# A hybrid SSD and attention block on one core: another order of rows in attention's second heads, and a later place for its first transposes

## The chip, the cores and the metric

The kernel runs on one core of one Trainium2 chip. The metric is the device time of one execution in microseconds. Three runs of the kernel before took 1223.24, 1229.5 and 1222.28 us; the median is 1223.24 us. One more execution was profiled.

## The reference, cut to what matters

One block of an encoder, on 1024 positions of width 1024, in float32:

```python
h = rms_norm(x, pre_mix_gain)
z, xbc, dt_raw, q, k, v = split(h @ w_in)              # 512, 1024, 8, 512, 512, 512 columns
xbc = silu(causal_depthwise_conv(xbc, conv_w, conv_b))  # 4 taps
y_ssd = gated_norm(ssd_scan(...) + d_skip * xs, z)      # 8 heads, a state of 128
# stick-breaking attention, 8 heads of 64; for each query block of 128 rows:
zz = q_block @ k[:end].T / 8
log_1mb = where(s < t, log_sigmoid(-zz), 0)
after = reverse_cumsum(log_1mb) - log_1mb
w = where(s < t, exp(log_sigmoid(zz) + after), 0)
o = w @ v[:end]
mix = concat([y_ssd, rms_norm_per_head(o)]) @ w_out
x = x + rms_norm(mix, post_mix_gain)
f = (silu(h2 @ w_gate) * (h2 @ w_up)) @ w_down          # h2 = rms_norm(x, pre_ffn_gain), width 2816
x = x + rms_norm(f, post_ffn_gain)
```

In attention a row of weights is as long as the positions that come before it, so the work of a query block grows with its place.

## The kernel before, in words

The sequence is reversed on the host, so that query block 0 has the longest rows (1024 keys) and block 7 the shortest (128). All large products are done in three passes of split operands (mm3, lines 77 to 79): high by high, high by low, low by high.

**Two streams.** The first part of the kernel runs two streams of work that one core shares. `fill` (line 887) projects the input: for each tile of 128 columns, `proj` (line 249) does two halves of 512 positions, each with 8 x 3 products, and gives way after every second of the 8 input blocks. At blocks 3 and 5 of the first half it fetches the next tile's weights (line 258). The order of tiles is PLAN: pair 1's q, k and v, then the conv tiles x0 to x5, pair 2's, x7, x6, the SSD recurrence (which runs beside), pair 3's, then the gates z and the first output loads. A conv tile also leaves four taps of work for VectorE to the side (lines 394 to 406), and it records the last product of each of its halves in the list `x_mm` (line 392).

`attention` (line 630) is the other stream. It has four pairs j of two heads h. A unit (j, h, g) is two neighbouring query blocks, 2g and 2g + 1: g = 0 has rows of 1024 and 896 keys, g = 1 of 768 and 640, g = 2 of 512 and 384, g = 3 of 256 and 128. For pairs 0 to 2 a head's units go from g = 0 to g = 3; in pair 3 the two heads alternate, from g = 3 to g = 0.

**One unit.** `weigh` (line 577) makes one row block of weights: products of q and k into zp (lines 589, 590), two sigmoids on ScalarE into sn and sp (591, 592), a mask on GpSimd (596), a running product along the row on VectorE (the scan, 597), and a product on VectorE (598) that leaves the weights in sp. `turn` (line 601) transposes the two rows' blocks on TensorE into tp (608); ScalarE copies that to wh (612) and VectorE takes the rest to wl (613). `mix_v` (616) multiplies by v into o. A unit has 4 - g turns, the first with 3 transposes, the others with 4. While unit i is turned, unit i + 1 is weighed: its first row in unit i's first turn, its second after the last turn. The first row of a new head first loads that head (`prep_head`, six loads on SyncE's queue), and for a new pair waits until that pair's v is emitted (`ready`, line 637). When a pair's last unit is done, `norm_o` (625) stores and squares its output.

**The order.** `merge` (line 690) takes from attention or from fill by a table of paces (PACE, line 43): attention goes on while its own count of VectorE work, as a share of A_ALL, is at or under the pace for the fill's count of TensorE work. A stream that gives way with (0, 0) has to wait, and the other goes on. What `merge` emits earlier has the higher priority; a scheduler then sets the final order on each engine by its own estimates, so an instruction that it takes for ready can be put ahead of one that it takes for waiting. On the chip each engine runs its own list in that order. `tc.issue_after(ins)` puts the instructions traced inside it, those on the engine of `ins`, behind `ins` in that engine's list. The second row of the first unit is already ordered so, behind the last product of x0's first half (line 656).

Of the kernel before, what the change touches and what calls it, by code (L numbers as in the profile page):

```python
# [47 lines left out]
def tile_hybrid_block(  # L48
# [20 lines left out]
    last_mm, evac, last_dve = [None], [None], [None]  # L69
# [6 lines left out]
    def mm3(ps, ah, al, bh, bl, start, stop, more=False):  # L76
        T.matmul(ps, lhsT=ah, rhs=bh, start=start, stop=False, skip_group_check=more)  # L77
        T.matmul(ps, lhsT=ah, rhs=bl, start=False, stop=False, skip_group_check=more)  # L78
        last_mm[0] = T.matmul(ps, lhsT=al, rhs=bh, start=False, stop=stop, skip_group_check=more)  # L79
# [9 lines left out]
    def psum(tag, name, shape=None, dt=F32):  # L89
        return psP.tile(shape or [P, 512], dt, tag=tag, name=name, bufs=BANKS[tag])  # L90
# [77 lines left out]
    def load_w_half(col, name, dh):  # L168
        raw = wp.tile([P, 4, P], F32, tag="wraw", name=f"wr_{name}", bufs=2)
        nc.sync.dma_start(raw, w_in_v[:, 4 * dh : 4 * dh + 4, col : col + P])  # L170
        hi = wp.tile([P, 4, P], F32R, tag="whi", name=f"wh_{name}")
        lo = wp.tile([P, 4, P], F32R, tag="wlo", name=f"wl_{name}")

        with tc.issue_after(first_sg[-1].ins) if name == "x1" else nullcontext():
            split(hi, lo, raw)
        return hi, lo
# [8 lines left out]
    def fetch_w(half=None):  # L185

        if cols:
            name, col = cols[0]
            w = w_tiles.setdefault(name, [])
            for dh in range(2) if half is None else (half,):  # L190
                w.append(load_w_half(col, name, dh))
            if len(w) == 2:
                cols.pop(0)

    def w_of(w, d):
        hi, lo = w[d // 4]
        return hi[:, d % 4, :], lo[:, d % 4, :]
# [51 lines left out]
    def proj(name, evac, dve):  # L249
        if name not in w_tiles:  # L250
            fetch_w()
        w = w_tiles.pop(name)
        for n in range(2):
            ps = psum("mm", f"pj_{name}")
            for d in range(ND):
                mm3(ps, *w_of(w, d), hh[d][n], hl[d][n], d == 0, d == ND - 1)
                if n == 0 and d in (3, 5):
                    fetch_w(d // 2 - 1)
                if d % 2 and d < ND - 1:
                    yield 1.3, 0  # L260
            evac(n, ps, slice(512 * n, 512 * n + 512))
            yield 1.3, dve
# [37 lines left out]
    v_first, k_evac, x_mm, decayed = [], [], [], []  # L300
# [245 lines left out]
    def prep_head(j, st, h):  # L546

        hsl = slice(64 * h, 64 * h + 64)
        kh = att.tile([P, S], F32R, tag="kh", name="kh")
        kl = att.tile([P, S], F32R, tag="kl", name="kl")  # L550
        qq = att.tile([P, S], F32R, tag="qq", name="qq")
        for half in range(2):
            dst = slice(64 * half, 64 * half + 64)
            nc.sync.dma_start(f32(qq[dst, :]), qkv_d[j]["q"][half][hsl, :])
        for half in range(2):
            dst = slice(64 * half, 64 * half + 64)
            nc.sync.dma_start(f32(kh[dst, :]), qkv_d[j]["k"][0][hsl, :])
            nc.sync.dma_start(f32(kl[dst, :]), qkv_d[j]["k"][1][hsl, :])
        return kh, kl, qq
# [17 lines left out]
    def weigh(head, qb):  # L577

        kh, kl, qq = head
        W = S - P * qb  # L580
        sn = att.tile([P, S + 1], F32, tag="sn", name="sn")
        sp = att.tile([P, S], F32, tag="sp", name="sp", bufs=3)
        G.memset(sn[:, 0:1], 1.0)
        off = 0
        qsl = slice(P * qb, P * qb + P)
        for cw_ in CH[W]:
            zp = psum("z", "zp", [P, 512])
            ksl = slice(P * qb + off, P * qb + off + cw_)
            T.matmul(zp[:, 0:cw_], lhsT=qq[:, qsl], rhs=kh[:, ksl], start=True, stop=False)
            T.matmul(zp[:, 0:cw_], lhsT=qq[:, qsl], rhs=kl[:, ksl], start=False, stop=True)  # L590
            A.activation(sn[:, 1 + off : 1 + off + cw_], zp[:, 0:cw_], AF.Sigmoid, scale=rqn[:, qb : qb + 1])  # L591
            sg = A.activation(sp[:, off : off + cw_], zp[:, 0:cw_], AF.Sigmoid, scale=rqp[:, qb : qb + 1])  # L592
            if len(first_sg) < 2:
                first_sg.append(sg)
            off += cw_
        G.affine_select(sp[:, 0:P], sp[:, 0:P], [[1, P]], ALU.is_gt, 0.0, base=0, channel_multiplier=-1)  # L596
        V.tensor_tensor_scan(sn[:, 1 : 1 + W], sn[:, 1 : 1 + W], smask[:, 0:W], 1.0, ALU.mult, ALU.max)  # L597
        V.tensor_tensor(sp[:, 0:W], sp[:, 0:W], sn[:, 0:W], ALU.mult)  # L598
        return sp

    def turn(ws, g, jj):

        kb = 2 * g + 2 * jj
        tp = psum("px", "tp", [P, 512])
        blocks = [(kb + 1, 0), (kb + 1, 1), (kb, 0)] + ([(kb, 1)] if jj else [])
        for i, (k, a) in enumerate(blocks):
            co = P * (k - 2 * g - a)
            T.transpose(tp[:, P * i : P * i + P], ws[a][:, co : co + P], ident)  # L608
        n_ = P * len(blocks)
        wh = att.tile([P, 512], F32R, tag="wh", name="wh", bufs=3)  # L610
        wl = att.tile([P, 512], F32R, tag="wl", name="wl", bufs=3)
        A.copy(wh[:, 0:n_], tp[:, 0:n_])  # L612
        V.tensor_tensor(wl[:, 0:n_], tp[:, 0:n_], f32(wh[:, 0:n_]), ALU.subtract)  # L613
        return kb, n_, wh, wl
# [10 lines left out]
    def norm_o(j, o_sb, n):  # L625
        sl = slice(512 * n, 512 * n + 512)
        nc.sync.dma_start(y_d[n][4 + j], o_sb[:, sl])
        mean_sq(o_sb[:, sl], sel2, 0, (j, j + 4), n, HD)

    def attention(st):  # L630


        units = [(j, h, g) for j in range(3) for h in range(2) for g in range(4)]
        units += [(3, h, g) for g in (3, 2, 1, 0) for h in range(2)]
        heads, vvs, osb, ws = {}, {}, {}, {}

        def ready(j):
            while "v" not in st[j] or not decayed:
                yield 0, 0

        def weights(i, a):
            if i < len(units):
                j, h, g = units[i]
                if (j, h) not in heads:
                    yield from ready(j)
                    heads[(j, h)] = prep_head(j, st[j], h)
                    yield 0, 0.1
                ws[(i, a)] = weigh(heads[(j, h)], 2 * g + a)
                W = P * (8 - 2 * g - a)
                yield W / 1200, W / 480 + 0.1  # L650

        yield from weights(0, 0)

        while not x_mm:
            yield 0, 0
        with tc.issue_after(x_mm[0].ins):
            yield from weights(0, 1)
        for i, (j, h, g) in enumerate(units):
            if j not in vvs:
                vvs[j] = prep_v(j, st[j])  # L660
                osb[j] = stg.tile([P, S], F32, tag="osb", name=f"osb{j}")
                yield 0.9, 1.2
            w = (ws.pop((i, 0)), ws.pop((i, 1)))
            o = psum("o", "o", [P, 256])
            n_j = 4 - g
            lag = None
            for jj in range(n_j):
                cur = turn(w, g, jj)
                yield 0.4, 0.6
                if jj == 0:  # L670
                    yield from weights(i + 1, 0)
                if lag is not None:
                    mix_v(o, vvs[j], h, lag, jj == 1, False)
                    yield 0.4, 0
                lag = cur
            yield from weights(i + 1, 1)
            mix_v(o, vvs[j], h, lag, n_j == 1, True)
            tmp = t2.tile([HD, 256], F32, tag="t2", name="otmp")
            A.copy(tmp, o[64:128, :])
            V.tensor_tensor(osb[j][64 * h : 64 * h + 64, 256 * g : 256 * g + 256], o[0:64, :], tmp, ALU.add)  # L680
            yield 0.4, 0.3
            if j < 3 and h == 1 and g == 3:
                norm_o(j, osb[j], 0)
                norm_o(j, osb[j], 1)
                yield 1.7, 0
            if j == 3 and h == 1 and g in (2, 0):
                norm_o(j, osb[j], g // 2)
                yield 0.9, 0
# [198 lines left out]
    def fill():  # L887
# [7 lines left out]
        yield from flush()  # L895

    merge(attention(st), fill())

    left_a.close()
# [427 lines left out]
    for p in range(last + 1):  # L1327
        while p not in done or done[p] < 7:
            pump(1 + LOOK)
            gate(step(p))  # L1330
            if p == last:
                i = done[p]
# [136 lines left out]
```

## Time and profile before

| what | value |
|---|---|
| median of three runs | 1223.24 us |
| profiled execution, its own time | 1221.82 us |
| its span, first to last instruction | 1220.1 us |
| TensorE busy | 1189.0 us, 97% |
| VectorE busy | 928.7 us, 76% |
| ScalarE busy | 588.9 us, 48% |
| mean granted clock of TensorE | 0.996 |

Attention's transposes run from 100.5 to 479.3 us of the span. Busy time counts an engine from the start to the end of its instructions, with overlaps once. A wait is named by the instruction that waited and by what released it. PE is TensorE, DVE is VectorE, ACT is ScalarE, POOL is GpSimd, SP is SyncE; L598 is line 598 of the kernel.

### The profile page before, as it was taken

The page shows a single profiled execution, that of the slowest core. Times are in us where ns is not written, and L with a number is a line of the kernel's source. Part 1 is how long each engine was busy: PE and PEld are TensorE (multiplying, and loading weights), DVE is VectorE, ACT ScalarE, POOL GpSimd, SP SyncE. Part 2 cuts the span into 40 slices and gives each one's busy share as a digit, 9 for nine tenths or more (in the row PEclk, how much of TensorE's full clock was granted, in tenths as well). Part 3 has the DMA queues.
Part 4 walks back from the last instruction along what each step waited for, and adds up shares of the span by engine and source line. Part 5 has one row for each costly group of instructions (what it writes and reads, how often), then busy time and mean ns, then how long its engine had stood idle before and what let it go on. Part 6 is the DMA issues. An engine that isn't in the chain of part 4 may idle for free.

```text
span 1220.1 us, 16382 instructions
## 1 busy us (share of the span) xinstructions
PE 1189.0 (97%) x5649; PEld 967.9 (79%) x5649; DVE 928.7 (76%) x1527; ACT 588.9 (48%) x1124; POOL 90.9 (7%) x232
## 2 busy tenths in 40 slices
PE   9999899999999998999999999999999999999997
PEld 7787777787887776688888888888888888888885
DVE  7468889778897988678898755566555559998877
ACT  7246656555654766455652323333233335444453
POOL 0011110101120100011200000000000000000000
PEclk9999999999999999999999999999999999999999
DMA  6794333445657424767963322322223397233246
GB/s 195 196 344 132 96 104 99 142 103 162 177 154 210 147 70 159 223 194 229 315 188 123 100 78 78 104 72 84 78 78 104 100 347 270 83 108 120 93 135 238
DMA packets 141414, 183.99 MB, mean 151 GB/s; under 512 B 10670, under 2 KB 96394, under 8 KB 141332
## 3 DMA queue, kind: packets, MB, share of 16 engines
q1 hardware_dynamic: 130016, 151.94, 40.8%
q0 software_dynamic: 7424, 25.17, 5.5%
q10 hardware_dynamic: 3892, 5.84, 1.3%
q8 instruction: 44, 0.72, 0.3%
q14 instruction: 38, 0.31, 0.1%
HBM read 133.00 MB, written 49.90 MB: 150 GB/s over the span
## 4 chain that ended last, share of the span: by engine, by line
PE 62%; DVE 5%; issue 2%; DMA 1%; ACT 1%; POOL 0%; SPq 0%; DVEq 0%; ACTq 0%; POOLq 0%
PE pd L78 5%; PE pd L77 5%; PE pd L79 5%; PE po L79 2%; PE po L78 2%; PE po L77 2%; PE peu L79 2%; PE pag L79 2%; PE peg L79 2%; PE pcu L79 2%; PE pcg L79 2%; PE pau L79 2%; PE pag L77 2%; PE pag L78 2%; PE pcg L77 2%
## 5 line engine op out<-in xcount | busy, mean ns | idle before, releaser
L73 ACT CAST flhi<-fraw 128x512 fp32r<-128x512 f32 x98 | 60.2, 622 | 153.4 <-PE pcg L78 36.6
L78 PE MATMUL pd<-folo,fohi 128*128 128x512 f32 x260 | 101.2, 389 | 0.0
L79 PE MATMUL pd<-fohi,folo 128*128 128x512 f32 x260 | 101.2, 389 | 0.0
L77 PE MATMUL pd<-fohi 128*128 128x512 f32 x260 | 101.2, 389 | 0.0
L597 DVE TENSOR_TENSOR_SCAN sn<-sn,smask 128x1024 f32<-128x1024 f32 (+3 forms) x64 | 87.4, 1365 | 17.9 <-ACT sn L591 17.4
L74 DVE TENSOR_TENSOR fllo<-fraw,flhi 128x512 fp32r<-128x512 f32 x98 | 66.8, 685 | 29.7 <-ACT flhi L73 29.7
L73 ACT CAST fohi<-rt 128x512 fp32r<-128x512 f32 x83 | 48.9, 618 | 49.1 <-PE pd L78 29.3
L591 ACT ACTIVATE sn<-zp,msc 128x512 f32<-128x512 f32 (+2 forms) x96 | 55.8, 584 | 33.1 <-PE zp L590 27.6
L612 ACT CAST wh<-tp 128x512 fp32r<-128x512 f32 (+1 forms) x80 | 43.3, 543 | 46.2 <-PE tp L608 45.3
L73 ACT CAST flhi<-fs 128x512 fp32r<-128x512 f32 x44 | 27.3, 622 | 67.9 <-PE peg L78 34.4
L608 PE MATMUL tp<-ident,sp 128*128 128x128 f32 x288 | 49.8, 278 | 10.5 <-DVE sp L598 9.5
L74 DVE TENSOR_TENSOR folo<-rt,fohi 128x512 fp32r<-128x512 f32 x83 | 55.0, 688 | 6.5 <-ACT fohi L73 6.5
L592 ACT ACTIVATE sp<-zp,msc 128x512 f32<-128x512 f32 (+2 forms) x96 | 55.7, 582 | 5.8 <-PE tp L608 4.1
L613 DVE TENSOR_TENSOR wl<-tp,wh 128x512 fp32r<-128x512 f32 (+1 forms) x80 | 49.7, 628 | 10.3 <-ACT wh L612 9.9
L78 PEld LDWEIGHTS pd<-folo,fohi 128*128 128x128 f32 x260 | 48.8, 188 | 10.3 <-DVE folo L74 0.3
L77 PEld LDWEIGHTS pd<-fohi 128*128 128x128 f32 x260 | 48.8, 188 | 10.2
L79 PEld LDWEIGHTS pd<-fohi,folo 128*128 128x128 f32 x260 | 48.8, 188 | 10.1
L77 PE MATMUL pj_x<-hh,wh_x 128*128 128x512 f32 x128 | 53.2, 416 | 0.0
L608 PEld LDWEIGHTS tp<-ident,sp 128*128 128x128 f32 x288 | 33.5, 140 | 24.7 <-DVE sp L598 14.5
L79 PE MATMUL po<-woh,yhl 128*128 128x512 f32 x128 | 49.9, 392 | 2.4 <-DVE yhl L74 2.4
L1064 POOL DMA_DIRECT2D a_d<-sg x44 | 23.8, 540 | 376.3 <-DVE sg L1063 376.2
L598 DVE TENSOR_TENSOR sp<-sp,sn 128x1024 f32<-128x1024 f32 (+3 forms) x64 | 48.2, 754 | 4.3 <-POOL sp L596 1.3
(435 smaller groups left out, 3482.4 us busy)
## 6 DMA issues: line engine op xcount, KB each, us to landing
ps<-a_d SPq DMA_DIRECT2D x55, 256.0 KB, 3.0
fraw<-in_w_gate_dram SPq DMA_DIRECT2D x22, 512.0 KB
fraw<-in_w_up_dram SPq DMA_DIRECT2D x22, 512.0 KB, 3.9
a_d<-sg POOLq DMA_DIRECT2D x44, 256.0 KB, 2.6
rt<-in_w_down_dram SPq DMA_DIRECT2D x33, 256.0 KB, 5.9
rt<-a_d SPq DMA_DIRECT2D x22, 256.0 KB, 4.2
ps<-in_w_down_dram SPq DMA_DIRECT2D x22, 256.0 KB, 3.0
xt<-in_x_t_dram SPq DMA_DIRECT2D x8, 512.0 KB, 4.9
```

Of the source, the lines that this page charges most:

```text
L73: A.copy(hi, src)
L74: V.tensor_tensor(lo, src, f32(hi), ALU.subtract)
L77: T.matmul(ps, lhsT=ah, rhs=bh, start=start, stop=False, skip_group_check=more)
L78: T.matmul(ps, lhsT=ah, rhs=bl, start=False, stop=False, skip_group_check=more)
L79: last_mm[0] = T.matmul(ps, lhsT=al, rhs=bh, start=False, stop=stop, skip_group_check=more)
L591: A.activation(sn[:, 1 + off : 1 + off + cw_], zp[:, 0:cw_], AF.Sigmoid, scale=rqn[:, qb : qb + 1])
L592: sg = A.activation(sp[:, off : off + cw_], zp[:, 0:cw_], AF.Sigmoid, scale=rqp[:, qb : qb + 1])
L597: V.tensor_tensor_scan(sn[:, 1 : 1 + W], sn[:, 1 : 1 + W], smask[:, 0:W], 1.0, ALU.mult, ALU.max)
L598: V.tensor_tensor(sp[:, 0:W], sp[:, 0:W], sn[:, 0:W], ALU.mult)
L608: T.transpose(tp[:, P * i : P * i + P], ws[a][:, co : co + P], ident)
L612: A.copy(wh[:, 0:n_], tp[:, 0:n_])
L613: V.tensor_tensor(wl[:, 0:n_], tp[:, 0:n_], f32(wh[:, 0:n_]), ALU.subtract)
```

## The change

Two things, independent of each other. First, in pairs 0 to 2 the second head's units go from g = 3 to g = 0; the first head's and all of pair 3's stay. The pair's norm moves with its last unit, which is now g = 0. Second, the first turn of the first unit is emitted only when `x_mm` has three entries, and its three transposes are ordered behind the third on TensorE. The third entry is new: it is the twelfth product of the first half of x1, recorded in `proj` (block 3); the first two remain the ends of x0's halves. Later entries of the list are used by nothing.

```diff
@@ proj
                 if n == 0 and d in (3, 5):
                     fetch_w(d // 2 - 1)
+                if name == "x1" and n == 0 and d == 3:
+                    x_mm.append(last_mm[0])
@@ attention
-        units = [(j, h, g) for j in range(3) for h in range(2) for g in range(4)]
+        units = [(j, h, g) for j in range(3) for h in range(2) for g in ((0, 1, 2, 3), (3, 2, 1, 0))[h]]
         units += [(3, h, g) for g in (3, 2, 1, 0) for h in range(2)]
...
             for jj in range(n_j):
-                cur = turn(w, g, jj)
+                while len(x_mm) < 3:
+                    yield 0, 0
+                with tc.issue_after(x_mm[2].ins) if i + jj == 0 else nullcontext():
+                    cur = turn(w, g, jj)
...
-            if j < 3 and h == 1 and g == 3:
+            if j < 3 and h == 1 and g == 0:
                 norm_o(j, osb[j], 0)
                 norm_o(j, osb[j], 1)
```

## The prediction

> **What bounds the kernel now.** I read the page first, then the waits of TensorE, then the stretches of the attention stage, and last the order of time around the largest wait. The page:
>
> ```profile
> span 1220.1 us, 16382 instructions
> ...
> PE 1189.0 (97%) x5649; PEld 967.9 (79%) x5649; DVE 928.7 (76%) x1527; ACT 588.9 (48%) x1124; POOL 90.9 (7%) x232
> ...
> PE 62%; DVE 5%; issue 2%; DMA 1%; ACT 1%; POOL 0%; SPq 0%; DVEq 0%; ACTq 0%; POOLq 0%
> ```
>
> TensorE is busy 1189.0 of 1220.1 us. The change adds and removes no arithmetic; it moves the order of what exists. So it can only move the 31 us in which TensorE stands, and whatever TensorE does at a low clock. The second view, TensorE's waits over the whole span, says who holds it (total, times, longest):
>
> ```profile
> PE tp L608 <- DVE sp L598: 9.5, 11, 2.3
> ...
> PE tp L608 <- POOL sp L596: 0.5, 1, 0.5
> ```
>
> The transposes of the attention weights (tp) wait 9.5 us in 11 waits for the last product of VectorE on a weight row (sp, line 598). That is the whole stake of the change in waits: under the 12.2 us that make one per cent of the time, which is about what a measurement of this kernel can tell from no change. The third view takes the stretches of the attention stage (busy us of each engine, then granted clock):
>
> ```profile
> core 0: us, PE busy (x) PEld busy (x) DVE busy (x) ACT busy (x) POOL busy (x), PEclk, DMA share, GB/s
> ...
> 97.30:118.50 21.20, 18.36 (x95) 15.07 (x93) 19.94 (x23) 13.10 (x24) 1.25 (x7) 0.92 0.25 71
> 98.00:180.00 82.00, 74.38 (x397) 61.33 (x396) 75.43 (x94) 49.93 (x91) 10.03 (x35) 0.98 0.32 86
> ...
> 104.20:107.70 3.50, 3.50 (x12) 2.73 (x11) 3.04 (x4) 1.80 (x4) 0.29 (x1) 0.51 0.30 80
> 180.00:260.00 80.00, 77.16 (x398) 62.51 (x397) 65.02 (x79) 47.88 (x88) 7.71 (x28) 1.00 0.43 126
> 260.00:400.00 140.00, 136.82 (x804) 112.59 (x803) 119.90 (x177) 79.73 (x172) 21.19 (x55) 1.00 0.57 164
> ```
>
> From 98 to 180 us VectorE is as loaded as TensorE: 75.43 against 74.38 of 82 us. This is the first head pair, where the conv tiles' taps run as well. From 180 on VectorE has 15 us free in 80. So one stage has two limits, and the rest of attention has one, TensorE. Around the largest wait the order of time on TensorE is (start, duration):
>
> ```profile
> 100.48 0.39 PE L79 MATMUL pj_x<-hh,wl_x 128*128 128x512 f32 x1
> 100.71 0.27 PE L608 MATMUL tp<-ident,sp 128*128 128x128 f32 x1
> ...
> 101.28 0.28 PE L589 MATMUL zp<-kh,qq 128*128 128x256 f32 x1
> 103.87 0.44 PE L608 MATMUL tp<-ident,sp 128*128 128x128 f32 x2 [2.31 <-DVE sp L598]
> ...
> 104.27 0.61 PE L77 MATMUL pj_x<-hh,wh_x 128*128 128x512 f32 x1
> ...
> 107.67 0.41 PE L79 MATMUL pj_x<-hh,wl_x 128*128 128x512 f32 x1
> ...
> 108.38 0.39 PE L79 MATMUL pj_x<-hh,wl_x 128*128 128x512 f32 x1
> ```
>
> The first turn of the first unit stands 2.31 us for its second weight row, although 12 products of x0 lie behind it in the queue and need nothing from attention. Then the clock falls: 8 products from 104.27 to 107.67 take 0.425 us each, the 3 from 107.67 to 108.38 take 0.237.
>
> **Part 2 of the change, the first transposes.** The turn (3 transposes) is emitted after the third entry of x_mm, and ordered behind it on TensorE. The first two entries come from the two halves of x0; the new one is the twelfth product of x1. From 101.28 that puts 24 products, 12 of x0 and 12 of x1, ahead of the turn: 24 x 0.235 = 5.6 us, so it starts at about 107 us, while the row it waited for is there at 103.9. The products need x1's weights, and their first half is split long before:
>
> ```profile
> 97.28 0.69 DVE L74 TENSOR_TENSOR wl_x<-wr_x,wh_x 128x512 fp32r<-128x512 f32 x1 [1.24 <-ACT wh_x L73]
> ...
> 104.33 0.68 DVE L74 TENSOR_TENSOR wl_x<-wr_x,wh_x 128x512 fp32r<-128x512 f32 x1
> ...
> 111.07 1.28 DVE L401 SCALAR_TENSOR_TENSOR cy<-u,pk,cy 128x1024 f32<-128x1024 f32 x1
> ...
> 385.23 0.69 DVE L290 TENSOR_TENSOR vr<-pj_v,R_b 128x512 f32<-128x512 f32 x1
> ...
> 392.21 0.69 DVE L597 TENSOR_TENSOR_SCAN sn<-sn,smask 128x256 f32<-128x256 f32 x1 [3.80 <-ACT sn L591]
> ```
>
> (VectorE in order of time; the last two rows are used further down.) What goes: the gap from 101.28 to 103.87, 2.59 us less the 0.12 that such a product needs, is 2.5 us; the half clock costs 8 x (0.425 - 0.237) = 1.5 us. Together 4.0 us on TensorE. [...]
>
> What is late next: the whole attention order. Emission of the turn, and of the weight rows of unit 1 behind it, slips by 12 products of x0 and x1 in the pace; the pace is then ahead of attention, which emits the turns of unit 0 in a row until it has caught up, about where unit 1 begins. In that time two or three taps of x0 (1.28 us each) go ahead on VectorE, and unit 1's scans come later. The load and split of x2's first half, which line 258 emits beside the twelfth product, now stand ahead of the turn in the emission; on SyncE's queue and on VectorE they already ran ahead of the turn's evacuation (104.33), so nothing is charged. GpSimd's memset and mask of a weight row move with that row and have no one else behind them here; it is busy 90.9 us of the span. Does VectorE let the 4.0 us through? In 97.3 to 118.5, up to the moment at which unit 1's rows are done, it is busy 19.94 of 21.20 us: the same work cannot end more than 1.26 us sooner. In the whole stretch to 180 it has 82 - 75.43 = 6.57 us. Of those, by VectorE's waits in 98 to 180:
>
> ```profile
> DVE wl L613 <- ACT wh L612: 2.4, 4, 0.8
> DVE sn L597 <- ACT sn L591: 1.1, 4, 0.3
> DVE u L391 <- PE pj_x L79: 1.0, 2, 0.7
> DVE cy L401 <- ACT cy L399: 0.7, 1, 0.7
> DVE sp L598 <- DVE sn L597: 0.2, 1, 0.2
> ```
>
> The 2.4 us is the handing over from a transpose through ScalarE and stays. The next three, 1.1 + 1.0 + 0.7 = 2.8 us, are waits for work that starts on TensorE (zp, pj_x) and shrinks when TensorE comes earlier. So I let 2.8 of the 4.0 us through. Ends: 0, if VectorE gives nothing, and 4.0, below VectorE's 6.57.
>
> **Part 1, the order in second heads.** Three heads are concerned (j = 0, 1, 2). Before, the step from a head's shortest unit to the next head's longest came with these waits (the first transposes of three units, from TensorE's order of time):
>
> ```profile
> 145.92 0.44 PE L608 MATMUL tp<-ident,sp 128*128 128x128 f32 x2 [1.90 <-DVE sp L598]
> ...
> 240.40 0.44 PE L608 MATMUL tp<-ident,sp 128*128 128x128 f32 x2 [0.98 <-DVE sp L598]
> ...
> 336.41 0.33 PE L608 MATMUL tp<-ident,sp 128*128 128x128 f32 x1 [0.18 <-ACT bs L444]
> ```
>
> These are 3.06 us, 1.02 a step. What is left of the waits on sp, 9.5 + 0.5 - 2.31 - 1.90 - 0.98 = 4.8 us, falls on the 18 shrinking steps: 0.27 each; nine of them, in the second heads, go, which is 2.4 us. Removed: 5.5 us. Added are three steps between equal short units, and nine to a longer unit. What a step asks of VectorE (groups of its instructions by shape from 98 to 400 us; after the bar stand the busy time in us and the mean ns of one, then the idle time before them):
>
> ```profile
> L613 DVE TENSOR_TENSOR wl<-tp,wh 128x512 fp32r<-128x512 f32 x36 | 24.1, 680 | 4.5 <-ACT wh L612 4.5
> ...
> L597 DVE TENSOR_TENSOR_SCAN sn<-sn,smask 128x896 f32<-128x896 f32 x6 | 12.3, 2047 | 0.0
> L597 DVE TENSOR_TENSOR_SCAN sn<-sn,smask 128x1024 f32<-128x1024 f32 x5 | 11.5, 2308 | 2.2 <-ACT sn L591 2.2
> ...
> L598 DVE TENSOR_TENSOR sp<-sp,sn 128x1024 f32<-128x1024 f32 x6 | 7.3, 1218 | 0.1
> L598 DVE TENSOR_TENSOR sp<-sp,sn 128x896 f32<-128x896 f32 x6 | 6.5, 1084 | 0.1
> ```
>
> The longest unit costs 2.308 + 2.047 + 1.218 + 1.084 = 6.66 us of VectorE, whichever unit stands before it. Before, that lay beside one turn; now the three turns of the unit before cover the first row, but the second row is still emitted just ahead of the turn that needs it. I price the three steps onto the longest unit at the old 1.02 (same last row, 3.1 us) and the other nine at 0.27 (2.4 us): added 5.5 us, net 0. Ends: all twelve at 0.27, net -2.2 us; all twelve at 1.02, 12.2 - 5.5 = +6.7 us.
>
> **What moves with it.** The next pair's head loads (SyncE's queue, six DMAs) and the wait for that pair's v are emitted in the first turn of the last unit, which now is the four-turn unit, with three turns behind it. Pair 1's v is projected before the first unit. Pair 2's last product of v ends before the first transposes of the last unit of pair 1 by 17 us:
>
> ```profile
> 253.56 0.40 PE L79 MATMUL pj_v<-hh,wl_v 128*128 128x512 f32 x1
> ...
> 271.11 0.49 PE L608 MATMUL tp<-ident,sp 128*128 128x128 f32 x3
> ```
>
> For pair 3 attention stands in any case: v3's second half is evacuated at 385.23 and the next scan of attention comes only then. Three turns now wait behind it: 3 evacuations of 0.68 us on VectorE, 2.0 us. Behind it VectorE stands 3.80 us before 392.21, which takes them in, and TensorE has the products of z0. I cost it at nothing; without that cover it would be 2.0 us. The loads:
>
> ```profile
> kh<-k_d SPq DMA_DIRECT2D x16, 256.0 KB, 4.9
> kl<-k_d SPq DMA_DIRECT2D x16, 256.0 KB, 6.5
> ```
>
> They land 4.9 to 6.5 us after issue (last column); three turns behind them cover more of that than none did. The norms of a finished pair still follow its last unit, and y_d is read only after attention. Nothing.
>
> **Sum.** -2.8 + 0 = -2.8 us. The profiled execution took 1221.82 us (span 1220.1), which gives 1219.0. It lies 1.42 under the median of the three runs, 1223.24; the forecast of the median is 1220.4.
>
> **Rivals.** *The wait only moves* (0.27): VectorE is the limit to 118.5, so the 2.3 us turn up a few us later, at the first turn of unit 1, whose rows VectorE ends no sooner than 1.26 us ahead of before. For it: 1.26 us of idle VectorE. Against: products of x1 and x2 can fill, and from 180 VectorE has room. Gain 0 to 1.3 us, middle 0.6: 1222.6. *Growing rows* (0.17, the other side): each step to a longer unit asks for more rows than the last unit's turns cover, and the twelve steps wait 1.02 us like the old steps from shortest to longest. +6.7 - 2.8 = +3.9 us: 1227.1. It turns the sign where the mean wait of the twelve steps passes (5.5 + 2.8)/12 = 0.69 us; a clock thrown once more adds 1.5. Against: those old steps had one turn of cover, and in the third pair the wait was 0.18. *The change does not act* (0.06): the transposes could be placed later by the edge, but the transposes' place on TensorE is no longer what is waited for, and something else (the first o product for its wl) stands there as long: 1223.2.
>
> The forecast has 0.50.
>
> **How the numbers follow.** The forecast's own range is the bounds: -2.2 - 4.0 = -6.2 to about -1, that is 1217.0 to 1222.2. The range takes in the moved wait and the growing rows up to their price: 1215.5 (all of VectorE's 6.57 us and half of part 1's -2.2) to 1227.1. Faster by over 1% would need 12.2 us, more than all waits on sp with the half clock (9.5 + 0.5 + 1.5 = 11.5): 0.02. Slower by over 1% needs the growing rows at their upper end with several thrown clocks: 0.04. The rest, 0.94, within 1%.
>
> **What would show it.** Right: no idle over 1 us before the first tp, a granted clock of 1.00 from 100 to 120 us, VectorE busier than 75.4 of the same 82 us, and the first turn at 105 to 108. Part 1 right: the waits before the first transposes of second heads' longest units near 1 us, others under 0.5. Wrong: a wait of 2 us or more at unit 1's first turn (the wait moved), or tp waiting on sp over 9.5 us in total (growing rows). A difference after 490 us would come from none of these steps.

## The result and the profile after

The changed kernel took 1228.04 us, the median of 16 runs (1223.96 to 1232.11); the kernel before took 1223.24 us, the median of 16 runs (1218.25 to 1229.5). The ratio is 1.0043, with a 95% interval of 1.0031 to 1.0054: about 5 us slower, half of one per cent. I had forecast 1220.4 us, 2.8 us faster, in a range of 1215.5 to 1227.1.

The profiled execution took 1229.76 us, 7.9 us more than that of before. The page of the kernel after:

```profile
span 1228.0 us, 16382 instructions
...
PE 1191.0 (97%) x5649; PEld 969.2 (79%) x5649; DVE 928.0 (76%) x1527; ACT 589.1 (48%) x1124; POOL 90.7 (7%) x232
...
PE 64%; DVE 2%; DMA 1%; ACT 1%; issue 1%; DVEq 0%; SPq 0%; ACTq 0%; POOL 0%
```

The instructions are the same in number. TensorE stands 1228.0 - 1191.0 = 37.0 us where it stood 31.1, 5.9 us more, and is busy 2.0 us longer for the same products, which is clock (granted 0.994 of full speed in the mean, against 0.996 before). In the chain that ended last VectorE's share fell from 5% to 2%. By the chain alone VectorE has left the path, and yet the time is longer.

What TensorE waits for over the whole span (total us, times, longest), after:

```profile
PE tp L610 <- DVE sp L600: 7.6, 12, 1.9
PE o L622 <- DVE wl L615: 5.7, 7, 1.2
PE pcb L439 <- DMA cx<-cx_d: 3.1, 2, 2.1
PE nps L513 <- ACT nsq L510: 3.1, 3, 1.6
```

And before:

```profile
PE o L620 <- DVE wl L613: 2.1, 4, 1.2
PE nps L511 <- ACT nsq L508: 2.0, 3, 1.6
...
PE pcb L437 <- DMA cx<-cx_d: 1.0, 1, 1.0
```

The wait of the transposes (tp) for their weight row, 9.5 us before, is down to 7.6. Three others grew by 3.6, 2.1 and 1.1 us: the products with v (o) for the second half of the transposed weights (wl), the SSD part's product pcb for its load, and the norm's product (nps) for the squares of a finished pair (nsq).

A milestone splits the 7.9 us. VectorE writes the output of a unit (osb) 32 times; the row gives the start of the first and of the last. After:

```profile
L687 DVE TENSOR_TENSOR osb<-o,otmp x32: 386/418/421, 117.8 to 494.0; 64x256 f32<-64x256 f32 x32
```

Before:

```profile
L680 DVE TENSOR_TENSOR osb<-o,otmp x32: 389/417/419, 119.6 to 487.6; 64x256 f32<-64x256 f32 x32
```

The first unit ends 1.8 us sooner, the last 6.4 us later. So 8.2 us are lost inside attention, behind its first unit, and only 7.9 - 6.4 = 1.5 us behind attention. Of the 1.8 us, 1.1 had come before anything that the change moves: attention's first scan begins at 92.66 us after and at 93.74 before. The last osb of each pair splits the loss further. It starts at 190.99, 285.79, 387.67 and 487.59 us before, and at 190.74, 288.09, 393.90 and 494.01 after. Pair 0 ends where it did, though attention began 1.1 us sooner; pair 1 takes 2.5 us longer, pair 2 takes 3.9 us longer and pair 3 0.2.

Where inside: three stretches of the middle of attention (the columns are those of the prediction's table of stretches). The outer two, 174 to 206 and 268 to 300 us, hold the ends of pair 0 and of pair 1. Before:

```profile
174.00:206.00 32.00, 31.44 (x160) 24.46 (x159) 28.41 (x34) 21.85 (x37) 2.41 (x11) 1.00 0.46 130
206.00:268.00 62.00, 59.35 (x317) 49.59 (x316) 47.88 (x65) 34.16 (x67) 7.08 (x25) 1.00 0.38 112
268.00:300.00 32.00, 31.99 (x158) 24.99 (x157) 27.79 (x32) 21.39 (x37) 3.65 (x8) 1.00 0.53 144
```

After:

```profile
174.00:206.00 32.00, 29.88 (x155) 23.24 (x153) 25.91 (x29) 18.90 (x33) 2.35 (x8) 1.00 0.27 85
206.00:268.00 62.00, 59.37 (x313) 49.58 (x314) 49.61 (x69) 35.46 (x70) 9.38 (x27) 1.00 0.47 132
268.00:300.00 32.00, 30.49 (x152) 23.73 (x151) 23.34 (x26) 18.61 (x32) 2.05 (x5) 1.00 0.32 91
```

At each of these two ends TensorE stands 1.5 us longer, 1.56 and 1.50; in the 62 us between, where the second head of pair 1 has its new order, it is as busy as before. And at the ends VectorE does less than before, 25.91 instead of 28.41 of 32 us, so it isn't short of time there.

What VectorE does at the end of pair 0 after the change, in order of time:

```profile
175.75 2.38 DVE L599 TENSOR_TENSOR_SCAN sn<-sn,smask 128x1024 f32<-128x1024 f32 x1
178.05 0.66 DVE L393 TENSOR_TENSOR u<-pj_x,R_b 128x512 f32<-128x512 f32 x1
178.63 1.21 DVE L600 TENSOR_TENSOR sp<-sp,sn 128x1024 f32<-128x1024 f32 x1
179.76 1.21 DVE L406 TENSOR_TENSOR cy<-cy,csg 128x1024 f32<-128x1024 f32 x1
180.90 1.27 DVE L615 TENSOR_TENSOR wl<-tp,wh 128x512 fp32r<-128x512 f32 x2
...
188.69 2.02 DVE L599 TENSOR_TENSOR_SCAN sn<-sn,smask 128x896 f32<-128x896 f32 x1
190.74 0.42 DVE L687 TENSOR_TENSOR osb<-o,otmp 64x256 f32<-64x256 f32 x1
```

And TensorE beside it:

```profile
155.01 0.62 PE L610 MATMUL tp<-ident,sp 128*128 128x128 f32 x2 [1.94 <-DVE sp L600]
...
171.13 0.44 PE L610 MATMUL tp<-ident,sp 128*128 128x128 f32 x2 [0.76 <-DVE sp L600]
...
181.63 0.38 PE L622 MATMUL o<-wl,vv 128*128 128x256 f32 x1 [1.01 <-DVE wl L615]
...
191.88 0.59 PE L513 MATMUL nps<-nsq,sel 128*2 128x512 f32 x1 [0.99 <-ACT nsq L510]
...
267.16 0.44 PE L610 MATMUL tp<-ident,sp 128*128 128x128 f32 x2 [0.60 <-DVE sp L600]
```

The last unit of a pair is now the long one, g = 0, with four turns. The rows of the next pair's first unit, also of 1024 and 896 keys, are weighed while it is turned. So the scan of 2.38 us and the product of 1.21 us stand, with two pieces of a conv tile between (u, cy), in VectorE's list ahead of the short wl (two take 1.27 us) that TensorE waits for at 181.63, and the second scan (2.02 us) stands ahead of the osb at 190.74 (0.42 us), which the norm waits for at 191.88. Nobody needs the two long rows yet.

The norm adds to it. `norm_o(j, …, 0)` squares the query blocks of g = 0 and 1 and goes first. Before, that half was complete two units ahead of the pair's end; after, it is the half that the last unit has just written. ScalarE's wait, with osb named:

```profile
191.19 0.63 ACT L510 ACTIVATE nsq<-osb 128x512 f32<-128x512 f32 x1 [2.20 <-DVE osb L687]
```

### The profile page after: what moved, and what is told of

Its sections match the earlier page's. It is cut to its first block, busy times and chain, and to the rows that moved or that the text cites. A ratio compares the mean times of both kernels' runs of the same rounds, so it can differ in the third digit from the quotient of the medians.

```text
span 1228.0 us, 16382 instructions
## 1 busy us (share of the span) xinstructions
PE 1191.0 (97%) x5649; PEld 969.2 (79%) x5649; DVE 928.0 (76%) x1527; ACT 589.1 (48%) x1124; POOL 90.7 (7%) x232
## 4 chain that ended last, share of the span: by engine, by line
PE 64%; DVE 2%; DMA 1%; ACT 1%; issue 1%; DVEq 0%; SPq 0%; ACTq 0%; POOL 0%
PE pd L79 5%; PE pd L77 5%; PE pd L78 5%; PE po L79 2%; PE po L77 2%; PE po L78 2%; PE pag L78 2%; PE pag L77 2%; PE pau L78 2%; PE peu L78 2%; PE peg L78 2%; PE pcu L78 2%; PE pcg L78 2%; PE pau L77 2%; PE peu L77 2%; PE peg L77 2%
## 5 line engine op out<-in xcount | busy, mean ns | idle before, releaser
L79 PE MATMUL po<-woh,yhl 128*128 128x512 f32 x128 | 50.6, 398 | 2.8 <-DVE yhl L74 2.8
L77 PE MATMUL po<-woh,yhl 128*128 128x512 f32 x128 | 51.2, 400 | 0.5 <-ACT yhl L73 0.5
L78 PE MATMUL pj_x<-hl,wh_x 128*128 128x512 f32 x128 | 51.3, 401 | 0.0
```

## The experiments

All of them compute the whole block and were timed in five rounds. Each ratio is to the kernel before, measured beside it. Since single executions of one kernel spread over some 10 us with the granted clock, I also give the difference at full clock, an estimate: the 113 runs of before beside the experiments, 1218.03 to 1229.4 us, follow 1217.4 us plus 1.05 us for every 0.001 that the mean granted clock lies under 1, so I took 1.1 us per 0.001 off each run and compared the means (two standard errors behind the ±). By that reckoning the change costs 1222.65 - 1217.15 = 5.5 us, so its loss isn't the clock's. (The 1217.15 us are the mean of those 113 runs, which were timed beside the experiments; the clocks of the 16 runs of before beside the changed kernel aren't on record.)

| kernel | ratio, 95% interval | mean clock, this / before | at full clock, us |
|---|---|---|---|
| e1, all three pairs' rows, nothing else | 1.0060 [1.0038, 1.0082] | 0.9946 / 0.9949 | +6.7 ± 0.8 |
| e2, first transposes, nothing else | 1.0009 [0.9993, 1.0025] | 0.9949 / 0.9949 | +0.9 ± 1.0 |
| e3, rows of pair 0 | 1.0025 [1.0006, 1.0044] | 0.9954 / 0.9949 | +3.3 ± 1.1 |
| e4, rows of pairs 1 and 2 | 1.0033 [1.0016, 1.0050] | 0.9944 / 0.9949 | +3.9 ± 1.0 |
| e5, e1 and the other half's norm first | 1.0027 [1.0009, 1.0044] | 0.9947 / 0.9944 | +3.3 ± 0.8 |
| e6, e1 and the next pair's row later | 1.0026 [1.0007, 1.0044] | 0.9939 / 0.9944 | +2.8 ± 0.8 |
| e7, second heads 2, 1, 0, 3 | 0.9974 [0.9958, 0.9989] | 0.9962 / 0.9944 | -1.4 ± 0.7 |
| e8, second heads 1, 2, 3, 0 | 1.0049 [1.0028, 1.0069] | 0.9939 / 0.9944 | +5.2 ± 1.0 |
| e9, e1 with both edits of e5 and e6 | 0.9989 [0.9975, 1.0004] | 0.9952 / 0.9937 | +0.8 ± 0.9 |
| e10, first transposes behind 12 products of x0 | 0.9989 [0.9975, 1.0004] | 0.9952 / 0.9937 | +0.1 ± 1.2 |
| e11, e7 and e10 together | 0.9971 [0.9958, 0.9984] | 0.9962 / 0.9937 | -1.2 ± 1.0 |
| e12, e2 and the taps after four turns | 0.9989 [0.9972, 1.0005] | 0.9951 / 0.9936 | -0.3 ± 1.1 |

**The two parts, each alone.** e1 takes only the order of the second heads:

```diff
-        units = [(j, h, g) for j in range(3) for h in range(2) for g in range(4)]
+        units = [(j, h, g) for j in range(3) for h in range(2) for g in ((3, 2, 1, 0) if h and j in (0, 1, 2) else (0, 1, 2, 3))]
...
-            if j < 3 and h == 1 and g == 3:
+            if j < 3 and h == 1 and g == (0 if j in (0, 1, 2) else 3):
```

> Only the second heads' order is changed (pairs 0 to 2); the first transposes stay where they were. Theory R (the rows cost, the first transposes gain a little that is kept): 4 to 8 us slower than the kernel before (ratio 1.0035 to 1.0065), and slower than the whole change or equal to it. Rival F (the first transposes' new place costs, since the turns then come in one bunch behind the taps): within 1.5 us of the kernel before. The first wait of 2.3 us at the first turn is back either way.

e2 takes only the first transposes:

```diff
+                if name == "x1" and n == 0 and d == 3:
+                    x_mm.append(last_mm[0])
...
-                cur = turn(w, g, jj)
+                while len(x_mm) < 3:
+                    yield 0, 0
+                with tc.issue_after(x_mm[2].ins) if i + jj == 0 else nullcontext():
+                    cur = turn(w, g, jj)
```

> Only the first transposes are moved behind the twelfth product of x1; the rows' order is the old one. Theory R: 0 to 3 us faster than the kernel before (0.9975 to 1.000): the trace of the changed kernel is about 5 us ahead at 105 us of its span and keeps part of that. Rival F: 3 to 6 us slower. In both, waits of o products on wl of about 1 us at 107 to 112 us, as in the whole change.

e1 took 1229.08 us against 1222.13, e2 1223.68, between the two ranges that I had set for it. The order of the rows costs all of the loss; the first transposes give nothing that can be measured. In e1 the ends of the pairs look as in the whole change: the two stretches have TensorE busy 29.73 and 30.48 us.

**The pairs, one by one.** e3 is e1 with `j in (0,)`, e4 with `j in (1, 2)`.

> Rows reversed in the second head of pair 0 alone, first transposes as before. If the rows cost where VectorE is full (98 to 180 us), this holds most of the rows' cost: 2.5 to 5 us slower than the kernel before. If each pair costs alike, 1.5 to 2.5 us slower.

> Rows reversed in the second heads of pairs 1 and 2 alone, first transposes as before. If VectorE's full stage is the cause, 0 to 2 us slower; if each pair costs alike (the long unit now stands before the next pair's long unit), 3 to 5 us slower, and with pair 0's kernel the two differences add up to that of all three pairs.

They took 1224.88 and 1226.43 us; their prices, 0.25% and 0.33%, add up to 0.58%, against e1's 0.60%. By size alone they decide nothing: e3's 2.75 us lies in the range for a cost that sits where VectorE is full, e4's 4.3 in that for pairs that cost alike. The place decides. What the stretches show of each pair's loss sits at that pair's own end. The stretches of e3, with the new order in pair 0 alone:

```profile
174.00:206.00 32.00, 29.99 (x155) 23.42 (x154) 25.91 (x28) 18.99 (x32) 2.33 (x8) 1.00 0.29 88
...
268.00:300.00 32.00, 32.00 (x160) 25.00 (x159) 27.58 (x32) 21.87 (x39) 4.10 (x9) 1.00 0.50 141
```

And of e4, with it in pairs 1 and 2:

```profile
174.00:206.00 32.00, 31.44 (x160) 24.41 (x159) 28.42 (x36) 21.55 (x37) 2.84 (x12) 1.00 0.43 125
...
268.00:300.00 32.00, 30.48 (x155) 23.84 (x154) 23.34 (x26) 19.20 (x32) 2.04 (x5) 1.00 0.31 91
```

The first stretch loses 1.45 us in e3 and nothing in e4; the second loses nothing in e3 and 1.51 us in e4. So the place, of that part of the loss, is the end of the pair. Two things are new there, and from here on I held two theories: the long unit that now ends the pair, and the steps from shorter to longer rows that lead up to it.

**Growing steps, or a long last unit.** e7 keeps growing steps (2, 1, 0) and ends the pair on the short unit, as before; e8 has shrinking steps (1, 2, 3) and ends it on the long one:

```diff
 e7:
+        units = [(j, h, g) for j in range(3) for h in range(2) for g in ((0, 1, 2, 3), (2, 1, 0, 3))[h]]
 e8:
+        units = [(j, h, g) for j in range(3) for h in range(2) for g in ((0, 1, 2, 3), (1, 2, 3, 0))[h]]
...
-            if j < 3 and h == 1 and g == 3:
+            if j < 3 and h == 1 and g == 0:
```

> Second heads in the order g = 2, 1, 0, 3: two steps to longer units as in the reversed order, but the pair ends on the short unit as before, so that its norm and the next pair's rows meet what they met before. Theory E: within 2 us of the kernel before (0.9985 to 1.0015). Rival G: 4 to 7 us slower (1.0035 to 1.0055).

> Second heads in the order g = 1, 2, 3, 0: two steps to shorter units as before and one from the shortest to the longest, but the pair ends on the long unit. Theory E: 3 to 6 us slower than the kernel before (1.0025 to 1.005). Rival G: within 1.5 us of it, since the one large step has only moved from the head's start to its end.

e7 took 1220.07 us and e8 1229.07, against 1223.94. The long last unit costs, with either kind of step before it; growing steps don't. e8 came out as theory E had it, e7 a little faster than that. The waits of e7 over the whole span show how little the one wait that I had taken for the stake says:

```profile
PE tp L608 <- DVE sp L598: 11.2, 13, 3.2
```

The transposes of e7 wait 11.2 us for their rows, against 9.5 before and 7.6 in the changed kernel, and e7 is the fastest of the three. Its two pair ends have TensorE busy 31.01 and 32.00 us, near those of before. That e7 is faster than before is measured (0.9974, interval to 0.9989); where its gain comes from isn't. About 2 us of it go with the clock, 0.9962 against 0.9944, the rest is the -1.4 us of the table.

**What at the pair's end.** e5 changes only the order of the two norms:

```diff
-                norm_o(j, osb[j], 0)
                 norm_o(j, osb[j], 1)
+                norm_o(j, osb[j], 0)
```

> The rows-only kernel (1.0060) with one more edit: at a pair's end the norm takes the half of g = 2 and 3 first, which is complete one unit earlier, then the half of g = 0 and 1 that the last unit has just written. Theory E (the cost sits at the pair's end: the long last unit meets the next pair's long rows on VectorE, and its norm waits for it): the waits of nps on nsq of 0.99 and 0.57 us after pairs 0 and 1 go, 1 to 2 us come back, ratio 1.004 to 1.0055. Rival G (the cost is the steps to longer units): no change, ratio 1.006.

e6 changes only the place of the next pair's first row, from the first turn of the last unit to its last turn:

```diff
-                if jj == 0:
+                if jj == (n_j - 1 if j < 3 and h == 1 and g == 0 else 0):
                     yield from weights(i + 1, 0)
```

> The rows-only kernel (1.0060) with one more edit: in a pair's last unit the first row of the next pair is emitted after the unit's last turn instead of after its first. Theory E: the waits of o products on wl of 1.02 and 0.95 us behind the scan of 1024 elements go, and 2 to 3 us come back: ratio 1.0035 to 1.0045. Rival G: ratio 1.006 or more, since nothing changes at the steps inside the head and the next pair's rows come later.

e5 took 1226.81 us and e6 1226.31, against 1223.94: each gives back about half of e1's loss, more than I had set for either. Their waits from 174 to 300 us tell two different stories. e5:

```profile
PE o L620 <- DVE wl L613: 2.0, 2, 1.0
```

e6:

```profile
PE nps L511 <- ACT nsq L508: 3.5, 2, 2.0
...
PE o L620 <- DVE wl L613: 0.5, 1, 0.5
```

With the norms swapped, the wait for nsq is gone and the o products still wait 2.0 us behind the long row. The half that is squared first is complete two units before the pair's end, not one as I had written. A new wait stands in e5 as well, 0.8 us of the products pv for a load, vld. With the row moved, the o products' wait falls from e1's 2.2 us to 0.5, and the norm's grows from 1.6 to 3.5: now the whole row stands between the last unit's products and its osb. In e6 the two stretches show no gain: TensorE is busy 29.95 and 29.97 us, the first at a granted clock of 0.95. What this profile wins against e1's lies behind them. From 300 to 420 us, where the third pair ends, TensorE is busy 116.89 us in e6, 115.32 in e1 and 116.49 before; but e9, with the same edit, has 114.83 there. So e6's half is known from its time, not from its waits. e9 makes both edits:

> The rows-only kernel with both edits at the pair's end: the norm's halves swapped and the next pair's first row after the last turn. Alone they gave 1.0027 and 1.0026 instead of 1.0060; with the second alone the nps waits grew to 2.04 and 1.43 us. If theory E holds the whole cost, the two add up: 0.999 to 1.0015, nps waits under 0.3 us, and no o wait near 1 us after pairs 0 and 1. If something else at the steps to longer units costs too (rival G in part), it stays at 1.002 or above.

It took 1223.47 us against 1224.15; the 1.0060 of e1 is back at 0.9989. The waits of e9 in 174 to 300 us:

```profile
PE nps L511 <- ACT nsq L508: 0.5, 1, 0.5
```

The o products no longer wait for wl, and the norm waits 0.5 us, a little over what I had set for it. The new order of rows itself, growing steps included, then costs nothing that can be measured (+0.8 ± 0.9 us at full clock), and it gains nothing either.

**The first transposes.** e10 takes the kernel before and puts the turn behind the second entry of x_mm, 12 products of x0, instead of 24 products of x0 and x1; e11 is e7 with the same edit.

```diff
+                while len(x_mm) < 2:
+                    yield 0, 0
+                with tc.issue_after(x_mm[1].ins) if i + jj == 0 else nullcontext():
+                    cur = turn(w, g, jj)
```

> The kernel before with its first transposes ordered behind the end of x0 (12 products ahead of them instead of 24), rows as before. Theory D (the wait removed comes back because attention falls behind the pace and then emits its turns in a bunch behind two taps): with half the delay the bunch is smaller, the first wait is under 0.6 us, the o waits on wl at 105 to 113 us are under 0.5 us, and 1 to 3 us are kept: ratio 0.9975 to 0.9992. Rival V (VectorE is full from 97 to 180 us, so whatever TensorE gains there is waited for later): ratio 0.9995 to 1.0015, as with 24 products (1.0009).

> Second heads in the order g = 2, 1, 0, 3 (0.9974) and the first transposes behind the end of x0. If the two are independent, 0.9974 times the ratio of the latter alone: 0.995 to 0.9966 by theory D, 0.997 to 0.999 by rival V.

e10 took 1221.94 us against 1224.15, e11 1220.59: neither stands apart from the kernel that it starts from. e10 was to tell two theories of part 2 apart, and did not: its ratio lies in theory D's range, but not the wait that D named. The first transposes wait 0.15 us, but the first o product with wl waits 0.84, over the 0.5 that D allowed. In e10's order of time:

```profile
104.87 0.39 PE L620 MATMUL o<-wl,vv 128*128 128x256 f32 x1 [0.84 <-DVE wl L613]
```

And on its VectorE:

```profile
104.26 0.55 DVE L613 TENSOR_TENSOR wl<-tp,wh 128x384 fp32r<-128x384 f32 x1
105.11 2.60 DVE L401 SCALAR_TENSOR_TENSOR cy<-u,pk,cy 128x1024 f32<-128x1024 f32 x2 [0.30 <-ACT cy L399]
```

Here the first wl stands ahead of the taps, and the first unit is shorter: from the start of its second scan to its first osb it takes 16.9 us (98.35 to 115.26), against 18.5 in e2 (98.35 to 116.86) and 19.4 before (100.22 to 119.60). The whole time keeps nothing of that which can be measured (+0.1 ± 1.2 us at full clock).

e12 takes e2 and keeps the taps of a conv tile back until attention has emitted four turns:

```diff
         def taps():
+            while len(turned) < 4:
+                yield 0, 0
...
+                turned.append(jj)
```

> The kernel with only the first transposes moved (24 products ahead; 1.0009), and the taps of the first conv tile emitted only after the four turns of the first unit. Theory D (what came back is the taps standing ahead of the turns' evacuations on VectorE): the waits of o on wl of 1.00 and 0.75 us at 107 to 112 us fall under 0.4 us together, nothing takes their place before 125 us, and about 1.5 us more are kept: ratio 0.9985 to 1.000. Rival V (VectorE is full there): those waits go, but the tp waits on sp of the next two units grow by as much, and the ratio stays at 1.0009 or above.

e12 took 1220.88 us against 1222.96, and its edit did not act. VectorE's order in e12 is that of the changed kernel, taps first:

```profile
105.26 2.60 DVE L405 SCALAR_TENSOR_TENSOR cy<-u,pk,cy 128x1024 f32<-128x1024 f32 x2 [0.78 <-ACT cy L403]
107.78 0.55 DVE L617 TENSOR_TENSOR wl<-tp,wh 128x384 fp32r<-128x384 f32 x1
```

The scheduler put the taps where they had been, although they were emitted later. So e12 is a second measurement of e2: +0.9 and -0.3 us at full clock, part 2 alone is worth nothing within 1 us. The taps behind all four turns were not tried; the nearest to it is e10, which has them behind the first wl.

## Why the prediction was wrong

**What bounds the kernel, and the stake: too narrow.** That the change can move only the time in which TensorE stands, and the clock, held: 5.9 us of standing and 2.0 of clock make the 7.9. But I took the wait of tp for sp as "the whole stake of the change in waits". That sum fell, by 1.9 us, while two others, of o for wl and of nps for nsq, rose by 4.7 us. A change of order moves every instruction that shares a list with those reordered; the stake is all waits on that list.

**Part 1, net 0: near, by prices that were wrong one by one.** Without the first wait of 2.31 us, tp waits 7.2 us for sp before and 7.6 after. The twelve new steps wait 0.35, 0.87, 1.94 and 0.76 us in pair 0 and 0.41, 0.42 and 0.60 in pair 1, and none is listed in pair 2: 5.4 us, where the sum had 5.5. The steps that went had waited 1.90 and 0.98 us and, in the second heads, 0.60, 0.51 and 0.45: 4.4 us, where the sum had 5.5. I had spread 4.8 us evenly over 18 steps, while every wait of tp for VectorE's sp lay before 260 us. So the steps cost about 1 us, near the 0 of the sum partly by luck; e7 and e9 bear out that it is little. The three steps onto the longest unit, which I had priced at 1.02 us, were cheaper: 0.76 us in pair 0 (171.13), 0.60 in pair 1 (267.16), none listed in pair 2. The dear one was a step from g = 2 to g = 1, 1.94 us at 155.01.

**What moves with it: the step that failed.** The pair's last unit, now of four turns, stood in the sum at nothing: "I cost it at nothing", for the three turns that wait behind pair 3's v, and "The norms of a finished pair still follow its last unit", with "Nothing" behind it. I had looked only at what the next pair's loads and v need, and whether three turns would wait for them. I didn't ask what the three turns wait for on VectorE: the next pair's long row, emitted in the first of them, stands ahead of their own wl. And I didn't ask which half the first norm reads. Those two cost 6.7 us together (e1), about half each (e5, e6), and taking away both takes away the loss (e9). Of the 6.7 us the profiles name 3 us, 1.5 us at each of the first two pair ends. The rest, among it the third pair, whose end lies among the SSD part's work, isn't located by a wait of its own. From 300 to 420 us, where that pair ends, TensorE is busy 1.6 us less after than before (114.87 and 116.49), but e9 has 114.83 there too, so this stretch settles nothing. The wait of pcb for its load, which grew by 2.1 us, isn't it: e9 has 2.2 us of it from 300 to 420 us, where before has 1.0, and its time is back.

**Part 2, 4.0 us taken out at the first turn: right in the profile. "I let 2.8 of the 4.0 us through": wrong, it was none.** The turn starts at 105.06 us, inside the 105 to 108 of the forecast, without the wait. The clock in the stretch that had 0.51 before, after the change:

```profile
104.20:107.70 3.50, 3.40 (x23) 2.79 (x21) 2.69 (x4) 2.95 (x5) 0.11 (x1) 1.00 0.55 140
```

Full clock, and 23 products in place of 12. What follows on TensorE:

```profile
105.06 0.49 PE L610 MATMUL tp<-ident,sp 128*128 128x128 f32 x3
...
109.15 0.38 PE L622 MATMUL o<-wl,vv 128*128 128x256 f32 x1 [1.13 <-DVE wl L615]
...
112.59 0.39 PE L622 MATMUL o<-wl,vv 128*128 128x256 f32 x1 [0.75 <-DVE wl L615]
```

And on VectorE, with ScalarE's copy of the same transposes behind it:

```profile
106.03 2.60 DVE L403 SCALAR_TENSOR_TENSOR cy<-u,pk,cy 128x1024 f32<-128x1024 f32 x2 [0.78 <-ACT cy L401]
108.55 0.55 DVE L615 TENSOR_TENSOR wl<-tp,wh 128x384 fp32r<-128x384 f32 x1
109.01 1.27 DVE L403 SCALAR_TENSOR_TENSOR cy<-u,pk,cy 128x1024 f32<-128x1024 f32 x1
110.21 1.75 DVE L599 TENSOR_TENSOR_SCAN sn<-sn,smask 128x768 f32<-128x768 f32 x1
111.87 0.67 DVE L615 TENSOR_TENSOR wl<-tp,wh 128x512 fp32r<-128x512 f32 x1
```

```profile
105.90 0.46 ACT L614 CAST wh<-tp 128x384 fp32r<-128x384 f32 x1
```

ScalarE had wh ready at 106.36. VectorE began two taps of x0 at 106.03, 2.60 us, and wl came at 108.55. So TensorE waits 1.13 and 0.75 us for VectorE a few us later, 1.9 of the 2.31 us. The 1.5 us of half clock come back elsewhere: e2 has the mean granted clock of before, 0.9949, and its profile has a granted clock of 0.50 from 142.8 to 146.2 us and of 0.99 in the mean from 300 to 420, where that of before has 0.51 from 49.6 to 53.1 and from 104.2 to 107.7, and 1.00 from 300 to 420. That VectorE and not the first transposes sets the end of this unit, e1 shows best: it still has the wait at the first turn (1.92 us, at 102.38), and yet ends its first unit at the same time as the changed kernel, whose osb row stands in the section on the result (117.8). In both profiles attention's first scan begins at 92.66 us. e1:

```profile
L680 DVE TENSOR_TENSOR osb<-o,otmp x32: 385/417/419, 117.6 to 491.8; 64x256 f32<-64x256 f32 x32
```

The bound that I had in hand, VectorE busy 19.94 of 21.20 us in 97.3 to 118.5, was the better figure; I then let a wider stretch, to 180 us, speak over it. There VectorE was to be busier than the 75.4 us of before; it was busy 74.88. And a better order of its list doesn't suffice either: e10's first unit is shorter, and its whole time isn't by anything that can be measured.

**The rivals.** For part 2, *the wait only moves* was right in kind, though the wait came not "at the first turn of unit 1" but at unit 0's own o products. That place stood in *the change does not act*, at 0.06: "the first o product for its wl". The transposes do come later here, as the edge says, and still that sentence describes part 2 best. *Growing rows*, at 0.17, named the right sign and nearly the right size (+3.9 us against 5 measured) by a mechanism that did not happen: tp waits on sp came to 7.6 us, under the 9.5 that were to be its mark, and growing rows with a short last unit (e7) are faster than before.

**The range and the chances.** The median missed the range by 0.9 us at its upper end, and lies within 1% of before, where I had put 0.94. The bounds held only the priced steps; what stood at nothing, the pair's end, had no upper bound of its own, and 6.7 us was what it came to in e1.

## What to carry to other kernels

When a loop of units is reordered, look first at its seams: what is emitted ahead of time for the next group, and whose results the closing step reads first. A long instruction that is early (a scan of 2.4 us) ahead of a short one that is due (an evacuation of 0.7 us) on the same engine made the fast engine wait here (1.01 us at 181.63), even where the slow one had time to spare; so end a group on its shortest unit, or, as e9 did, move the early work behind the group's last turn and let the closing step read first what is complete first. Either edit of e9 alone gave back only half. And before a removed wait is booked as gain, read what stands in the list of the engine that the next wait names.

## What I had not expected of the hardware

Behind waits of one length TensorE's granted clock fell in one execution and not in another. In the changed kernel, behind the 1.94 us at 155.01 shown above:

```profile
155.10:158.50 3.40, 3.40 (x10) 2.72 (x11) 1.88 (x3) 2.59 (x4) 1.24 (x3) 0.50 0.18 68
```

In e1 the same turn, after a wait as long, had the full clock behind it:

```profile
155.36 0.44 PE L608 MATMUL tp<-ident,sp 128*128 128x128 f32 x2 [1.95 <-DVE sp L598]
```

```profile
155.40:158.80 3.40, 3.40 (x16) 2.87 (x17) 3.16 (x4) 2.60 (x4) 1.27 (x3) 1.00 0.20 75
```

Half clock for 3.4 us against full clock, 10 products against 16, behind 1.94 and 1.95 us of idle. Other waits differ in the same way: behind 1.90 us, at 142.63, e2 has 0.50 from 142.8 to 146.2 us; behind 1.92 us, at 102.38, e1 starts its next products of x0 0.23 us apart, as at full clock. So between 1.90 and 1.95 us the length of the wait doesn't tell whether the clock falls behind it; what does is not shown.

So a single profiled execution carries a few us of chance. The profiled spans of before and after lie 7.9 us apart where the medians lie 4.8 apart. Over the 16 runs of the changed kernel the time goes with the mean granted clock, from 1223.96 us at 0.997 to 1231.79, the mean of two runs, at 0.993.
